# Class 0's V rows gathered per token and summed on TensorE; its routing kept on chip; classes 1 and 2 routed one after the other

## The chip, the core and the metric

One core of one Trainium2 chip runs the kernel. The time is the device time of one execution, in microseconds (us). Engines are named as in the profile: PE is TensorE, DVE is VectorE, ACT is ScalarE, POOL is GpSimd, SP is SyncE.

## The reference

One layer over 512 tokens of width 1024: a token-mixing part, then a channel-mixing part that looks up neurons by product keys (PEER), then a last RMSNorm. All in float32. Cut to what matters here:

```python
h = rmsnorm(x, norm_mix_g); proj = h @ w_in          # u/v gating, q for 3 patterns, k, v, two gates
y_a = spatial_gating_mixer(gelu(u, v)); y_b = dilated_attention_mixer(q, k, v)
x = x + (sigmoid(gate_a) * (y_a @ w_branch_a) + sigmoid(gate_b) * (y_b @ w_branch_b)) @ w_out
h2 = rmsnorm(x, norm_ffn_g)
s = scores of h2 @ w_q against 8 heads x 2 x 128 sub-keys
top_s, top_i = top_k(s, 16)                          # per half; 16 x 16 sums, again top_k 16 per head
expert, gate = 8 heads x 16 experts of 16384 and their softmax, per token
act = gelu(u_tab[expert] . h2) * gate                # 128 rows of 1024 per token
x = x + sum_k act[k] * v_tab[expert[k]]              # 128 rows of 1024 per token
out = rmsnorm(x, norm_final_g)
```

## The kernel before

**Classes.** The 512 tokens are split by t mod 4 into four classes of 128 tokens, one token a partition. Class 0 goes through the whole mixing part first and alone, with plain float32 matmuls (`exact=True`). Classes 1 to 3 follow together, with each operand split into two parts (`split`, L83 to 85) and three matmuls instead of one (`mm`, L102 to 108).

**Two ways to do the PEER part.** Classes 1 and 2 (`ND = 2`) are done densely: all 16384 experts' activations are made on PE (`up_pair`, 128 tiles of 128 experts, `gelu` on ACT), multiplied by a gate matrix that is zero where an expert wasn't chosen, and summed with V on PE into PSUM tiles `acc`. The gate matrix is built by `gates` from one-hot matmuls and goes through DRAM (`g_dram`, read back as `gl`). Classes 0 and 3 are done by gathers (`gathered`): for each of a token's 128 experts one indirect DMA, issued by POOL (L251), brings 128 rows of 4 KB, one for each token, into one of seven `row` buffers. For U, DVE multiplies the row by h2 and sums it (L266); for V, DVE adds the row, scaled by its activation, to `xg` (L259). Both classes are 256 gathers each.

**Routing.** `route` finds one chunk's (two heads') 16 best experts on DVE: top 16 of 128 twice for each head, 50 sums, top 16 of them, and three instructions on 800 elements to look up the expert's number. Four chunks make a class. Classes 0 and 3 write their scores to DRAM (`s_dram`) and `gathered` reads them back; classes 1 and 2 are routed within the loop over scores, chunk by chunk, both classes in turn (`route_of`).

**Order.** `gathered` is a generator, and each `yield` is a step. The two classes make one list: 36 steps of routing, 256 gathers, and again the same for class 3. The 36 of class 0 are emitted ahead of the attention of classes 1 to 3. All later ones are emitted by `gather_steps(us, behind)`, which the projections, the heads, the up tiles and the V loop call behind one of their instructions with the PE time of their piece: it takes `us * rate` steps. `rate` is MIX (0.5) up to the scores, and then what is left of 549 steps over the time of the up tiles and the V loop. `tc.issue_after` puts a step's instructions behind the given one on that one's engine. A planner that simulates the program then fixes each engine's order; every engine runs its own list in that order.

**Stages.** x, norm, transposes to hT (two buffers for `h`); projections z, k, v; class 0's attention, gating, merge, residual, scores; then, for classes 1 to 3, `attention`, `gating`, `merge`, `residual`, `scores` with routing. Then the up tiles ahead of time: 40 kept in SBUF (`pre`), 20 spilled to `a_dram` (`NSP`), beside `gates` for both classes at a high priority. Then the V loop over 128 tiles in pairs: the other 68 up tiles, gl, the product, four float32 matmuls for the first tile of a pair and twelve split ones for the second. `finish` norms each class and stores it. Tile names in rows: `pj` a projection's PSUM, `po` the attention's output (64 of 128 columns a head), `tr` a transpose, `pu_t` an up tile, `pg` a gates tile, `h_dram`, `s_dram`, `x_dram` the tensors in DRAM.

Of the kernel before, what the change touches and what calls it, by code (L numbers as in the profile page):

```python
# [19 lines left out]
P = 128  # L20
# [3 lines left out]
D = 1024  # L24
# [10 lines left out]
NSP = 20  # L35
# [6 lines left out]
GPB = 7  # L42
STEPS = 549
MIX = 0.5
WUS = 4.2
HUS = 4.5
UUS = 3.43
# [4 lines left out]
def body(ctx, tc, a, out):  # L52
# [21 lines left out]
    s_dram = [dp.tile([4, P, 4, P], F32, name=f"s_dram{i}") for i in range(2)]  # L74
    h2_dram = [dp.tile([P, D], F32, name=f"h2_dram{i}") for i in range(2)]
# [25 lines left out]

    def mm(ps, l, r, first, last):  # L102
        if len(l) == 1:
            nc.tensor.matmul(ps, l[0], r[0], start=first, stop=last)  # L104
# [3 lines left out]
        nc.tensor.matmul(ps, l[1], r[0], start=False, stop=last)  # L108
# [120 lines left out]
    def gathered(gp, i, r):  # L229

        h2g = gp.tile([P, D], F32, tag="h2g", name="h2g", bufs=1)
        nc.sync.dma_start(h2g, h2_dram[i])
        xg = gp.tile([P, D], F32, tag="xg", name="xg", bufs=1)
        nc.sync.dma_start(xg, x1_dram[r])
        bv = gp.tile([P, 8, 16], F32, tag="bv", name="bv_g", bufs=1)
        ef = gp.tile([P, 8, 16], F32, tag="ef", name="ef_g", bufs=1)
        for c in range(4):
            sg = gp.tile([P, 4, P], F32, tag="sg", name="sg", bufs=1)
            nc.sync.dma_start(sg, s_dram[i][c])
            yield from route(gp, sg, bv[:, 2 * c:2 * c + 2, :], ef[:, 2 * c:2 * c + 2, :],  # L240
                             lambda: gp.tile([P, D], F32, tag="row", name="eq", bufs=GPB)[:, 0:16 * NC].rearrange(
                                 "p (k n) -> p k n", k=16))
        eidx = gp.tile([P, P], I32, tag="eidx", name="eidx", bufs=1)
        gate = gp.tile([P, P], F32, tag="gate", name="gate", bufs=1)
        nc.vector.tensor_copy(eidx, ef.rearrange("p h k -> p (h k)"))
        softmax16(bv, gate)
        pend = []

        def row_of(table, k):
            row = gp.tile([P, D], F32, tag="row", name="row", bufs=GPB)  # L250
            nc.gpsimd.indirect_dma_start(out=row, out_offset=None, in_=table,  # L251
                                         in_offset=bass.IndirectOffsetOnAxis(ap=eidx[:, k:k + 1], axis=0))
            return row

        def down():
            k0, act = pend.pop(0)
            for k in range(GB):
                row = row_of(a["v"], k0 + k)
# [3 lines left out]
        for k0 in range(0, P, GB):  # L262
            ab = gp.tile([P, GB], F32, tag="ab", name="ab", bufs=2)
            for k in range(GB):
                row = row_of(a["u"], k0 + k)
                nc.vector.scalar_tensor_tensor(row, row, 1.0, h2g, op0=ALU.mult, op1=ALU.mult,  # L266
                                               accum_out=ab[:, k:k + 1])
                yield
# [9 lines left out]

    ph = ExitStack()
# [3 lines left out]
    with ExitStack() as p1:  # L283
        pp = pool(p1, "pp", 4, space=PSUM)
        pst = pool(p1, "pst", 1, space=PSUM)
        ptr = pool(p1, "ptr", 1, space=PSUM)
        pv = pool(p1, "pv", 1, space=PSUM)
# [28 lines left out]
        pa = ExitStack()  # L316
        pha = ExitStack()
        hap = pool(pha, "hap", side="right")
        hA = Op(hap, [P, KT, P], "hA", True)
        with ExitStack() as p0:  # L320
# [67 lines left out]
        aw = pool(pa, "aw", 2, reuse_waits="tile")  # L388

        def attention(pl, cl, x, ybT, exact, hook):  # L390
# [10 lines left out]
            def heads(hp):  # L401
                q1, q2 = q_of(hp)
                po = pv.tile([P, 512], F32, tag="pv", name="po")
                for j, r in enumerate(cl):
                    tok = slice(j * P, j * P + P)
                    for hh in range(2):
# [8 lines left out]
                        sm = aw.tile([P, 768], F32, tag="sm", name="sm")  # L415
                        mx = sp.tile([P, 1], F32, tag="mx", name="mx")
                        nc.vector.tensor_tensor_reduce(out=sm, in0=s[:, 0:768], in1=bias[:, j, :], scale=1.0,
# [4 lines left out]
                        pr = aw.tile([P, 768], F32, tag="pr", name="pr")  # L422
                        nc.scalar.activation(pr, sm, AF.Exp, bias=nb, scale=slope, accum_out=den)
# [9 lines left out]
                        pt = aw.tile([P, 4, P], F32, tag="pt", name="pt")  # L433
# [61 lines left out]
        def residual(pl, cl, mT, exact, hook):  # L495
# [10 lines left out]
            for j, r in enumerate(cl):  # L506
                nc.sync.dma_start(x1_dram[r], x1[:, j, :])
                h2 = pl.tile([P, D], F32, tag="h2", name="h2")
# [4 lines left out]
        def scores(pl, x, n, each, exact, hook):  # L513
            for c in range(4):
                skc = pl.tile([P, 4, P], F32, tag="sk", name="skc")
# [13 lines left out]
        def to_dram(pl, i):  # L529
            def each(c, j, ps):  # L530
                ssb = pl.tile([P, 4, P], F32, tag="ssb", name="ssb")
                nc.scalar.copy(ssb, ps)
                nc.sync.dma_start(s_dram[i][c], ssb)
            return each


        with ExitStack() as ga:
# [5 lines left out]
            m_ = pool(ga, "mA", 2, reuse_waits="tile")  # L543
# [4 lines left out]
            for r, h2 in residual(m_, [0], mT, True, 0):  # L548
                nc.sync.dma_start(h2_dram[0], h2)
                for q in range(2):  # L550
                    t = transpose4([h2[:, (4 * q + i) * P:(4 * q + i + 1) * P] for i in range(4)])
                    h2A.put((slice(None), slice(4 * q, 4 * q + 4), slice(None)), t)
            scores(m_, lambda kt: h2A[:, kt, :], P, to_dram(m_, 0), True, 0)
# [258 lines left out]
```

## Time and profile before

| | us |
|---|---|
| median of three runs (1855.36 to 1861.1) | 1859.0 |
| the profiled execution | 1855.0 |
| its span, first to last instruction | 1853.2 |
| PE busy, weight loads busy, DVE busy | 1651.0, 1345.7, 1300.8 |
| ACT busy, POOL busy | 548.2, 689.5 |
| moved by DMA | 552.5 MB, 298 GB/s on the mean |

Busy times are of instructions and overlap between engines. A busy PE isn't a PE at its peak: a matmul at the half clock takes twice as long. The time between the span and the execution, 1.8 us, lies around the first and last instruction.

### The profile page before, as it was taken

Reading aid. Unit: us, or ns where it says so; the run is one execution under the profiler, and the core shown is the slowest. Engines: PE = TensorE matmul, PEld = TensorE weight load, DVE = VectorE, ACT = ScalarE, POOL = GpSimd, SP = SyncE. Lnnn points to the kernel's source line nnn. Section 1 sums busy time; section 2 is a strip of 40 time slices with the busy share of each in tenths; the row PEclk is TensorE's granted clock in tenths of the full one; section 3 lists DMA queues with packets and bytes.
Section 4 is the critical chain, followed back from the end, with each engine's and each line's share of the span. In section 5 each row is a group of like instructions: output and inputs, shape, how many; then the busy total and the mean of one; then the engine's idle time right before and its main releaser. Section 6 shows DMA issues by size and latency. Waiting matters only on the chain.

```text
span 1853.2 us, 22603 instructions
## 1 busy us (share of the span) xinstructions
PE 1651.0 (89%) x7838; PEld 1345.7 (73%) x7838; DVE 1300.8 (70%) x2749; ACT 548.2 (30%) x1045; POOL 689.5 (37%) x535
## 2 busy tenths in 40 slices
PE   7999989988779977889999865899998999999997
PEld 6988969876679957888779753455566667677675
DVE  3333014999899988999999964687775656667564
ACT  4324113443333323311048694112211111111111
POOL 0000000007676655354555000574453454455350
PEclk9999999995699987999999977999999999999999
DMA  5235777219899998879899735999998999999995
GB/s 201 91 106 167 274 245 281 86 53 329 298 338 378 364 353 328 299 281 368 324 360 383 268 129 198 388 406 379 377 395 315 356 373 357 374 382 406 364 358 195
DMA packets 166914, 552.54 MB, mean 298 GB/s; under 512 B 17296, under 2 KB 38800, under 8 KB 165648
## 3 DMA queue, kind: packets, MB, share of 16 engines
q1 hardware_dynamic: 93072, 282.63, 42.1%
q0 software_dynamic: 73728, 268.47, 38.6%
q8 instruction: 62, 1.02, 0.2%
q14 instruction: 52, 0.43, 0.1%
HBM read 524.29 MB, written 26.74 MB: 297 GB/s over the span
## 4 chain that ended last, share of the span: by engine, by line
PE 45%; DVE 22%; issue 15%; DMA 12%; POOL 3%; ACT 2%; SPq 0%; POOLq 0%; DVEq 0%; ACTq 0%
PE pu_t L632 10%; DVE row L266 6%; PE pj L104 6%; PE acc L104 5%; PE pj L108 5%; PE pj L106 5%; PE pj L107 5%; DMA raw<-in_v_dram 4%; DVE xg L259 3%; POOL row L251 3%; DMA row<-in_u_dram,eidx 2%; PE acc L107 2%; PE acc L108 2%; DMA row<-in_v_dram,eidx 2%; PE acc L106 2%
## 5 line engine op out<-in xcount | busy, mean ns | idle before, releaser
L251 POOL DMA_INDIRECT row<-in_u_dram,eidx x256 | 334.1, 1305 | 525.0 <-DVE pr L429 157.9
L251 POOL DMA_INDIRECT row<-in_v_dram,eidx x256 | 343.1, 1340 | 326.5 <-DVE xg L259 133.7
L632 PE MATMUL pu_t<-h2T,raw 128*128 128x256 f32 x2048 | 456.0, 381 | 5.2 <-DMA raw<-in_ut_dram 3.8
L632 PEld LDWEIGHTS pu_t<-h2T,raw 128*128 128x128 f32 x2048 | 390.0, 191 | 62.5 <-issue 6.6
L259 DVE SCALAR_TENSOR_TENSOR xg<-row,act,xg 128x1024 f32<-128x1024 f32 x256 | 327.9, 1281 | 7.9 <-DMA row<-in_v_dram,eidx 4.6
L266 DVE SCALAR_TENSOR_TENSOR row<-row,h2g 128x1024 f32<-128x1024 f32 x256 | 305.8, 1216 | 17.0 <-DMA row<-in_u_dram,eidx 16.8
L85 DVE TENSOR_TENSOR wlo<-raw,whi 128x1024 fp32r<-128x1024 f32 x88 | 107.1, 1218 | 111.0 <-ACT whi L84 110.8
L104 PE MATMUL acc<-raw,ge 128*128 128x512 f32 x352 | 162.6, 605 | 12.3 <-DMA raw<-in_v_dram 12.3
L84 ACT CAST whi<-raw 128x1024 fp32r<-128x1024 f32 x88 | 92.4, 1050 | 223.1 <-PE pj L107 134.2
L104 PEld LDWEIGHTS acc<-raw,ge 128*128 128x128 f32 x352 | 68.0, 194 | 80.8 <-issue 70.6
L106 PE MATMUL acc<-vh,ah 128*128 128x512 f32 x256 | 116.9, 489 | 8.6 <-ACT vh L84 5.3
L143 POOL TENSOR_TENSOR rs<-ms,mhalf 128x1 f32<-128x1 f32 x16 | 11.4, 717 | 303.6 <-DVE ms L141 303.6
L107 PE MATMUL acc<-vl,ah 128*128 128x512 f32 x256 | 107.5, 423 | 18.4 <-DVE vl L85 18.4
L633 ACT ACTIVATE ge<-pu_t 128x256 f32<-128x256 f32 x68 | 26.0, 383 | 314.0 <-PE pu_t L632 313.9
L106 PE MATMUL pj<-hT_hi,whi 128*128 128x384 f32 (+1 forms) x320 | 114.2, 357 | 4.6 <-ACT u L462 3.6
L107 PE MATMUL pj<-hT_lo,whi 128*128 128x384 f32 (+1 forms) x320 | 112.7, 352 | 0.0
L85 DVE TENSOR_TENSOR vl<-raw,vh 128x1024 fp32r<-128x1024 f32 x64 | 78.2, 1222 | 49.1 <-ACT vh L84 48.1
L108 PE MATMUL pj<-hT_hi,wlo 128*128 128x384 f32 (+1 forms) x320 | 100.6, 357 | 11.6 <-DVE wlo L85 11.5
L108 PE MATMUL acc<-vh,al 128*128 128x512 f32 x256 | 102.5, 408 | 0.9 <-DVE al L85 0.9
L666 PE MATMUL pg<-hot 128*128 128x128 f32 x512 | 74.9, 307 | 31.4 <-ACT stg L669 21.0
L84 ACT CAST vh<-raw 128x1024 fp32r<-128x1024 f32 x64 | 66.8, 1043 | 116.4 <-DMA raw<-in_v_dram 114.5
L666 PEld LDWEIGHTS pg<-hot 128*128 128x128 f32 x512 | 70.5, 216 | 36.6 <-ACT stg L669 29.8
(215 smaller groups left out, 2651.7 us busy)
## 6 DMA issues: line engine op xcount, KB each, us to landing
raw<-in_ut_dram SPq DMA_DIRECT2D x128, 512.0 KB, 6.6
raw<-in_v_dram SPq DMA_DIRECT2D x128, 512.0 KB, 7.1
raw<-in_w_in_dram SPq DMA_DIRECT2D x88, 512.0 KB, 4.1
raw<-in_wq_dram SPq DMA_DIRECT2D x32, 512.0 KB, 5.7
g_dram<-stg SPq DMA_DIRECT2D x8, 2048.0 KB, 7.2
gl<-g_dram SPq DMA_DIRECT2D x32, 512.0 KB, 8.3
raw<-in_wa_dram SPq DMA_DIRECT2D x16, 512.0 KB, 5.5
raw<-in_wo_dram SPq DMA_DIRECT2D x16, 512.0 KB, 5.1
```

Of the source, the lines that this page charges most:

```text
L84: nc.scalar.copy(hi, src)
L85: return nc.vector.tensor_tensor(lo, src, hi.bitcast(F32), ALU.subtract)
L104: nc.tensor.matmul(ps, l[0], r[0], start=first, stop=last)
L106: nc.tensor.matmul(ps, l[0], r[0], start=first, stop=False)
L107: nc.tensor.matmul(ps, l[0], r[1], start=False, stop=False)
L108: nc.tensor.matmul(ps, l[1], r[0], start=False, stop=last)
L251: nc.gpsimd.indirect_dma_start(out=row, out_offset=None, in_=table, in_offset=bass.IndirectOffsetOnAxis(ap=eidx[:, k:k + 1], axis=0))
L259: nc.vector.scalar_tensor_tensor(xg, row, act[:, k:k + 1], xg, op0=ALU.mult, op1=ALU.add)
L266: nc.vector.scalar_tensor_tensor(row, row, 1.0, h2g, op0=ALU.mult, op1=ALU.mult, accum_out=ab[:, k:k + 1])
L632: nc.tensor.matmul(ps, raw[:, kt * P:kt * P + P], h2T.t[0][:, kt, :], start=kt == 0, stop=kt == KT - 1)
L633: last = nc.scalar.activation(dst(k), ps, AF.Gelu)
L666: nc.tensor.matmul(ps[:, m, :], hot[1][:, 4 * q + m, :], hot[0][:, 4 * q + m, :], start=True, stop=True)
```

## The change

Class 0 gets a generator of its own, `gathered_pe`. Its U rows are gathered as before (128 steps). Then the activations and expert numbers are transposed on PE, so that a token's 128 experts lie on the partitions, and a V gather brings the 128 rows of *one token*. Its sum over experts is a matmul with one column of weights; four tokens, one of each quarter of 32 columns, make a group: weights `ex` of 32 columns with one column filled, four tokens, two halves of 512 columns, eight float32 matmuls, accumulated over 32 groups in PSUM. Class 0's scores are copied into a row buffer and routed chunk by chunk within its own loop over scores. Class 1 is routed in the loop over scores, class 2 (`late`) between the gates of class 1 and of class 2. Class 3 keeps the old way, with all its steps in the V loop. Steps are put behind the last matmul on PE as well. Buffers: eight row buffers instead of seven, one `h` buffer in the first stage, `sm` and `pr` of the attention one tile, 12 spilled up tiles instead of 20, the pools of PSUM for the attention closed after it to make room for `acc_A`. The diff, cut:

```diff
-NSP = 20
+NSP = 12
-GPB = 7
-STEPS = 549
-MIX = 0.5
+GPB = 8
+MIX = 0.53
+PUS = 4.4
...
-        with tc.issue_after(behind.ins):
+        with tc.issue_after(behind.ins), tc.issue_after(on_pe.ins):
...
+    def gathered_pe(bv, ef, h2g, r):
+        eidx = gp.tile([P, P], I32, tag="eidx", name="eidx")
+        gate = gp.tile([P, P], F32, tag="gate", name="gate")
+        e = ef.rearrange("p h k -> p (h k)")
+        nc.vector.tensor_copy(eidx, e)
+        softmax16(bv, gate)
+        act = gp.tile([P, P], F32, tag="ab", name="act")
+        yield from u_rows(eidx, h2g, act, 0, P)
+        nc.scalar.activation(act, act, AF.Gelu)
+        nc.vector.tensor_tensor(act, act, gate, ALU.mult)
+        ps = v_acc()
+        nc.tensor.transpose(ps[:, 0:P], act, ident)
+        nc.tensor.transpose(ps[:, P:2 * P], e, ident)
+        actT = gp.tile([P, P], F32, tag="gate", name="actT")
+        nc.scalar.copy(actT, ps[:, 0:P])
+        eT = gp.tile([P, P], I32, tag="eidx", name="eT")
+        nc.vector.tensor_copy(eT, ps[:, P:2 * P])
+        pend = []
+        def down():
+            n, rows, ex = pend.pop(0)
+            for f in range(2):
+                for j in range(4):
+                    c = slice(f * 512, f * 512 + 512)
+                    nc.tensor.matmul(ps[32 * j:32 * j + 32, c], ex[:, j, :], rows[j][:, c], start=n == 0, stop=n == 31)
+        for n in range(32):
+            ex = gp.tile([P, 4, 32], F32, tag="ex", name="ex", bufs=3)
+            one = iota[:, 0:32].unsqueeze(1).to_broadcast([P, 4, 32])
+            nc.vector.scalar_tensor_tensor(ex, one, float(n), actT[:, n:P:32].unsqueeze(2).to_broadcast([P, 4, 32]),
+                                           op0=ALU.is_equal, op1=ALU.mult)
+            rows = []
+            for j in range(4):
+                rows.append(row_of(a["v"], eT[:, 32 * j + n:32 * j + n + 1]))
+                if j == 3 and pend:
+                    down()
+                yield
+            pend.append((n, rows, ex))
+        xg = load_x(r)
+        down()
+        for q in range(2):
+            f = slice(q * 512, q * 512 + 512)
+            nc.vector.tensor_tensor(xg[:, f], xg[:, f], ps[:, f], ALU.add)
+        finish(gp, r, xg)
...
+    NA, NCL = 256, 292
...
-                h = x0.tile([P, D], F32, tag="h", name="h")
+                h = x0.tile([P, D], F32, tag="h", name="h", bufs=1)
...
-                        sm = aw.tile([P, 768], F32, tag="sm", name="sm")
+                        pr = pl.tile([P, 768], F32, tag="pr", name="pr", bufs=3)
...
+            def route_A(c, j, ps):
+                sg = in_row("sg", 4, P)
+                nc.scalar.copy(sg, ps)
+                for _ in route(gp, sg, bvA[:, 2 * c:2 * c + 2, :], efA[:, 2 * c:2 * c + 2, :], row_eq):
+                    pass
...
+        steps = gathered_pe(bvA, efA, h2A_n, 0)
...
+        pat.close()
+        pva = ExitStack()
+        acc_A.append(pool(pva, "pva", 1, side="right", space=PSUM, reuse_waits="tile").tile([P, D], F32, name="acc_A"))
...
         def route_of(c, j, ps):
...
-            if j < ND:
-                for _ in route(l2, ssb, bvs[j][:, 2 * c:2 * c + 2, :], efs[j][:, 2 * c:2 * c + 2, :],
+            if j == 0:
+                route_now(j, c, ssb)
+            elif j == 1:
+                late.append((j, c, ssb))
             else:
-                nc.sync.dma_start(s_dram[1][c], ssb)
+                nc.sync.dma_start(s_dram[c], ssb)
...
-    rate = (STEPS - taken) / (P * UUS + P // 2 * sum(VUS) - LATE)
+    npre = len(KEPT) + len(SPILLED)
+    rate = (NA - taken) / (2 * npre * PUS - LATE)
...
         for r in range(ND):
+            if r == 1:
+                for args in late:
+                    route_now(*args)
             g = l2.tile([P, P], F32, tag="g", name="g")
...
     pr_.close()
+    for _ in steps:
+        pass
+    pva.close()
+    pacc = pool(ctx, "pacc", 1, space=PSUM, reuse_waits="tile")
+    steps = gathered(3)
+    rate = NCL / ((P - 2 * npre) * UUS + P // 2 * sum(VUS) - LATE)
```

## Rows read from the trace of the kernel before

**Rows 1.** The page's parts 1 and 2: busy times; the span in 40 slices.

```profile
PE 1651.0 (89%) x7838; PEld 1345.7 (73%) x7838; DVE 1300.8 (70%) x2749; ACT 548.2 (30%) x1045; POOL 689.5 (37%) x535
...
DVE  3333014999899988999999964687775656667564
...
GB/s 201 91 106 167 274 245 281 86 53 329 298 338 378 364 353 328 299 281 368 324 360 383 268 129 198 388 406 379 377 395 315 356 373 357 374 382 406 364 358 195
```

**Rows 2.** Windows by stage: length, busy PE, PEld, DVE, ACT, POOL, clock, DMA share, GB/s.

```profile
297.00:489.00 192.00, 165.12 (x852) 140.83 (x852) 169.58 (x556) 73.47 (x121) 57.10 (x46) 0.82 0.56 193
489.00:655.00 166.00, 152.54 (x813) 146.87 (x812) 154.93 (x208) 59.59 (x78) 110.38 (x77) 0.97 0.94 344
655.00:712.00 57.00, 34.86 (x128) 25.71 (x127) 45.15 (x61) 16.07 (x23) 30.51 (x25) 0.72 0.96 358
712.00:1056.00 344.00, 323.16 (x1698) 294.65 (x1697) 340.74 (x1025) 126.44 (x277) 159.96 (x114) 0.97 0.88 325
1056.00:1131.00 75.00, 46.30 (x267) 40.39 (x265) 47.66 (x81) 67.94 (x164) 0.00 (x0) 0.82 0.39 153
1131.00:1160.00 29.00, 16.39 (x43) 9.10 (x44) 17.16 (x41) 4.16 (x7) 0.67 (x1) 0.70 0.78 259
1160.00:1836.00 676.00, 634.15 (x2307) 440.77 (x2306) 444.05 (x619) 113.55 (x200) 324.02 (x257) 0.98 0.97 370
```

**Rows 3.** Waits: who waited for whom, us in total, times, the longest.

```profile
DVE pre L718 <- DMA gl<-g_dram: 20.4, 2, 19.7
```

**Rows 4.** Windows of the instructions on tile row alone: DVE, POOL, clock, DMA share, GB/s.

```profile
297.00:489.00 192.00, 47.47 (x71) 57.10 (x46) 0.82 0.56 193
...
489.00:1131.00 642.00, 268.93 (x313) 296.00 (x210) 0.93 0.85 313
```

**Rows 5.** Groups by line: busy us, mean ns of one, idle before.

```profile
L148 ACT ACTIVATE h<-xt 128x1024 f32<-128x1024 f32 x4 | 4.3, 1064 | 4.5 <-DMA xt<-in_x_dram 4.5
...
L259 DVE SCALAR_TENSOR_TENSOR xg<-row,act,xg 128x1024 f32<-128x1024 f32 x256 | 327.9, 1281 | 7.9 <-DMA row<-in_v_dram,eidx 4.6
...
L200 DVE TENSOR_TENSOR eq<-eq,cande 128x800 f32<-128x800 f32 x32 | 30.7, 979 | 0.0
...
L157 DVE MAX8 tv<-rep 128x8 f32<-128x128 f32 x64 | 17.8, 279 | 0.1
...
L661 ACT ACTIVATE hot<-hot,tt 128x128 f32<-128x128 f32 x256 | 78.3, 389 | 17.9 <-DVE hot L658 17.9
...
L669 ACT COPY stg<-pg 128x512 f32<-128x512 f32 x64 | 62.7, 1057 | 6.7 <-PE pg L666 6.6
```

**Rows 6.** Timeline of PE and DVE at the start: start, us, instruction, idle before it.

```profile
5.59 0.15 DVE L141 TENSOR_SCALAR ms<-ss 128x1 f32<-128x1 f32 x1 [4.74 <-ACT h L148]
...
7.82 1.97 PE L292 MATMUL tr<-ident,h 128*128 128x128 f32 x8 [7.82 <-DVE h L331]
...
19.25 1.94 PE L292 MATMUL tr<-ident,h 128*128 128x128 f32 x8 [2.50 <-DVE h L331]
```

**Rows 7.** Timeline of ACT, DVE and POOL from 268 to 415.

```profile
272.51 0.58 ACT L532 COPY ssb<-ps 128x512 f32<-128x512 f32 x1 [2.50 <-PE ps L526]
...
296.54 1.22 DVE L85 TENSOR_TENSOR wlo<-raw,whi 128x1024 fp32r<-128x1024 f32 x1 [38.50 <-ACT whi L84]
...
309.52 0.88 DVE L154 MAX8 tv<-sg 128x8 f32<-128x128 f32 x4 [1.03 <-DMA sg<-s_dram]
...
414.63 1.13 POOL L251 DMA_INDIRECT row<-in_u_dram,eidx  x1 [157.91 <-DVE pr L429]
```

**Rows 8.** Chain that ended last, in order of time: start, us, what.

```profile
447.27 2.29 DVE row L266 x4
...
1208.99 3.43 PE acc L104 x8
...
1360.58 3.45 PE pu_t L632 x16
```

**Rows 9.** Timeline of PE in the attention.

```profile
359.14 1.09 PE L436 MATMUL po<-pt,v_sb 128*64 128x128 f32 x8
```

More of the change, by code (lines that the diff above doesn't have):

```diff
@@ L100, in __getitem__ @@
             return [t[at] for t in self.t]
+    on_pe = None
     def mm(ps, l, r, first, last):
+        nonlocal on_pe
         if len(l) == 1:
-            nc.tensor.matmul(ps, l[0], r[0], start=first, stop=last)
+            on_pe = nc.tensor.matmul(ps, l[0], r[0], start=first, stop=last)
             return
@@ L107, in mm @@
         nc.tensor.matmul(ps, l[0], r[1], start=False, stop=False)
-        nc.tensor.matmul(ps, l[1], r[0], start=False, stop=last)
+        on_pe = nc.tensor.matmul(ps, l[1], r[0], start=False, stop=last)
     steps = iter(())
@@ new lines, in in_row, with row_eq, routed, load_x @@
+    def in_row(name, k, n):
+        row = gp.tile([P, D], F32, tag="row", name=name, bufs=GPB)
+        return row[:, 0:k * n].rearrange("p (k n) -> p k n", k=k)
+    def row_eq():
+        return in_row("eq", 16, NC)
+    def routed():
+        return [gp.tile([P, 8, 16], F32, tag=t, name=t + "_g") for t in ("bv", "ef")]
+    def load_x(r):
+        xg = gp.tile([P, D], F32, tag="xg", name="xg")
+        nc.sync.dma_start(xg, x1_dram[r])
+        return xg
+    def u_rows(eidx, h2g, ab, k0, n):
+        for k in range(n):
+            row = row_of(a["u"], eidx[:, k0 + k:k0 + k + 1])
+            nc.vector.scalar_tensor_tensor(row, row, 1.0, h2g, op0=ALU.mult, op1=ALU.mult, accum_out=ab[:, k:k + 1])
+            yield
@@ L245, in gathered @@
+    def gathered(r):
+        h2g = gp.tile([P, D], F32, tag="h2g", name="h2g")
+        nc.sync.dma_start(h2g, h2_dram)
+        bv, ef = routed()
+        for c in range(4):
+            sg = in_row("sg", 4, P)
+            nc.sync.dma_start(sg, s_dram[c])
+            yield from route(gp, sg, bv[:, 2 * c:2 * c + 2, :], ef[:, 2 * c:2 * c + 2, :], row_eq)
+        eidx = gp.tile([P, P], I32, tag="eidx", name="eidx")
+        gate = gp.tile([P, P], F32, tag="gate", name="gate")
         nc.vector.tensor_copy(eidx, ef.rearrange("p h k -> p (h k)"))
@@ L246, in gathered @@
         softmax16(bv, gate)
+        xg = load_x(r)
         pend = []
[L249 to L253, printed above, removed]
         def down():
@@ L262, in gathered @@
         for k0 in range(0, P, GB):
[L263 to L268, printed above, removed]
+            ab = gp.tile([P, GB], F32, tag="abk", name="ab", bufs=2)
+            yield from u_rows(eidx, h2g, ab, k0, GB)
             act = gp.tile([P, GB], F32, tag="act", name="act", bufs=3)
@@ L277, in gathered @@
         yield
+    NA, NCL = 256, 292
+    gp = pool(ctx, "gp", 1, side="right", reuse_waits="tile")
     ph = ExitStack()
@@ L547, in body, with v_acc @@
             h2A = Op(ya_, [P, KT, P], "h2A", True)
[L548 to L549 removed]
+            for r, h2A_n in residual(m_, [0], mT, True, 0, lambda: gp.tile([P, D], F32, tag="h2g", name="h2g")):
                 for q in range(2):
[L551 removed]
+                    t = transpose4([h2A_n[:, (4 * q + i) * P:(4 * q + i + 1) * P] for i in range(4)])
                     h2A.put((slice(None), slice(4 * q, 4 * q + 4), slice(None)), t)
[L553 to L564 removed]
+            bvA, efA = routed()
+            def route_A(c, j, ps):
+                sg = in_row("sg", 4, P)
+                nc.scalar.copy(sg, ps)
+                for _ in route(gp, sg, bvA[:, 2 * c:2 * c + 2, :], efA[:, 2 * c:2 * c + 2, :], row_eq):
+                    pass
+            scores(m_, lambda kt: h2A[:, kt, :], P, route_A, True, 0)
+        acc_A = []
+        def v_acc():
+            return acc_A[0]
+        steps = gathered_pe(bvA, efA, h2A_n, 0)
         GROUP = [1, 2, 3]
```

95 lines of the change are left out of this document (36 added, 59 removed).

## The prediction

> **What bounds the kernel now.** I read the page first: TensorE (PE) is busy 89% of the span, VectorE (DVE) 70%, and neither share says which of them ends a stage. The slices, 46.3 us each and counted from 0, do [rows 1]: DVE stands at 8 or 9 from slice 7 to slice 22 and mostly at 4 to 7 after that; the DMA engines move 280 to 406 GB/s from slice 9 on, except in slices 22 to 24 and the last.
>
> The stages by windows [rows 2] are then, in us from the span's start. 297 to 489, attention of classes 1 to 3: DVE 169.6 busy of 192, PE at a mean clock of 0.82. 489 to 655, gating and merge: DVE 154.9 and PE 152.5 of 166, both nearly full. 655 to 712, residual: neither is full (PE 34.9, DVE 45.2 of 57); the chain x1, sum of squares, rs, h2, transposes runs in series. 712 to 1056, scores, routing, up tiles, the first gates: DVE 340.7 of 344, PE 323.2. 1056 to 1131: a tail in which ScalarE scales and stores the gates, 67.9 of 75, while PE does 46.3 and no gather is issued. 1131 to 1836, the V loop: first 29 us with PE at 16.4, a wait of 19.7 us for the first gl [rows 3] in it, then PE 634 of 676 with the DMA engines at 0.97 and 370 GB/s.
>
> So DVE sets the time from 297 to 1056, the gates on ScalarE set it to 1131, and PE and DMA share it after that. GpSimd's count [rows 4] puts 46 gathers before 489 and 210 before 1131: 256, so all of class 0 lie there and all of class 3 behind.
>
> **The change, part by part.** The sum is made against the profiled execution, 1855.0 us, of which the span is 1853.2; the median of the three runs, 1859.0, lies 4 us above it, so I give the sum and add 1 to 2.
>
> *Start.* With one h buffer the square of the next class, which writes its junk there, waits for the transposes of the one before. Now the four classes' transposes start from 7.82 to 19.25, 3.8 apart on the mean. In series a class costs its square, 1.06 [rows 5], from ms to the transposes 7.82 - 5.59 = 2.23, the transposes 1.97 [rows 6], and gaps, 5.6; the last starts near 24.7, and nothing hides it, since the first projection needs all classes: +5.5 (between 0 and +9).
>
> *Class 0's routing, in SBUF.* It loses the trip of the scores through DRAM and starts when the first chunk is copied out, at 273.1, not at 309.5; DVE has been idle for 38.5 us by then [rows 7]. One chunk of routing is six instructions on 800 elements (0.98 each), twenty on 128 (0.28, [rows 5]), and some forty smaller ones that I put at 0.08 to 0.2: 17 us, a class 68. About 24 us of it move into idle DVE time, and the gathers, which begin at 414.6, begin near 360.
>
> *Attention.* Its DVE work was 169.6 = 47 for rows [rows 4] + 68 routing + 54 of its own. It becomes 44 + 54 + rows. The hooks of this stage (12 of 4.2 us, 24 of 4.5) ask for 158.4 x 0.53 = 84 u rows at 1.15 (2.29 for two rows, [rows 8]) = 97, so 195 of DVE work where 170 was: it ends near 495, not 489, but with 84 rows done where 46 were. +6. If the rows slide later it gains, see the rivals. The merged sm and pr tile costs nothing: three buffers where two of each stood, and DVE is the limit beside it.
>
> *The V sums.* 128 instructions of 1281 ns leave DVE [rows 5], 164 us by the mean, 147 as they pack. What comes is 32 small ones on 128 elements, 0.28 each by the nearest row, 9 us, and a few evacuations. From 489 to 1131 DVE had 588 us of work; without the 147, the 68 of class 3's routing and the 43 of the 37 rows that come earlier, and with the 9, some 340 are left, so DVE is no bound there. What is late next is PE: each group of four tokens adds 8 float32 matmuls of 512 columns, 16 passes, since a float32 matmul is issued as two (eight passes in 3.43 for four matmuls, 0.429 a pass, [rows 8]). Every matmul behind them on PE's queue waits, and a group whose rows are late would hold the projections; with 8 row buffers a group's gathers are issued one group (4 steps, 7.5 us at 0.53) before they are needed, and a row's 0.5 MB passes in 1.4 us at the stage's 370 GB/s, four in 5.6. I take that as covered.
>
> The price of a group isn't in the trace. The nearest rows are the attention's po, matmuls on one half of the columns: eight passes of 128 columns in 1.09 [rows 9], 0.107 a pass by the columns (0.429 / 4), so a narrower block is not faster, plus about 0.2 around it. They all follow one another in the same half, so they don't say whether different quarters run beside each other. Bounds: all 16 passes in turn, 6.86 + 0.2 = 7.06 a group, 226 us in all; four quarters side by side, 4 passes, 1.72 + 0.2 = 1.92, 61.5 us. I take the low end: the matmuls of the four quarters share neither columns, weights nor output rows, and PE does run what shares nothing side by side, weight loads 73% of the span beside matmuls of 89% [rows 1]. Both ends are kept for the range.
>
> The Trainium skill (TensorEngine Tiling (Array Packing), Theoretical Speedup) gives up to 4 times for at most 32 columns; by it a group is 6.86 / 4 = 1.72 and the whole 55, an estimate that no run here shows yet.
>
> *489 to 1131.* PE is busy 557 of 642 in the four stages summed [rows 2], idle 85. Idle that goes, because DVE no longer ends these stages: 20.8 from 712 to 1056, 28.7 in the gates' tail, 10 of 13.5 in gating and merge; and about 10 from the half clock of the tail (46.3 busy at 0.82). The tail goes because class 1 alone is routed beside the scores (68 where 136 were), its gates run under the up tiles, and class 2 is routed beside them. ScalarE's chain, twice 85 (16 rounds a class, eight scalings of 0.39 and two copies of 1.06 each, [rows 5], 5.2 a round), then ends near 1030, inside the up tiles. The residual's 22 stays. Sum -70. Eight up tiles fewer (NSP 12): 8 x 3.45 [rows 8] = -28, moved to the V loop. The V groups +62. Together -36: the V loop starts near 1106.
>
> *V loop.* +28 for the eight up tiles; -20 for the wait for gl, which now finds the gates written. It still holds 256 gathers, but class 3's routing (36 steps at 292 / 641 = 0.456 a us) takes its first 79 us, in which no row is asked for and the loads draw about 190 GB/s. The bytes were 250 + 7.5 MB [rows 2]; eight more ut loads and eight fewer spilled tiles make 261. 15 of them pass in the first 80 us, 246 in the rest, at 390 GB/s (between the stage's 370 and the 406 of its best slice, [rows 1]) 630: 710 where 705 were, +5. PE's own work, 634 + 16 + 28 = 678, lies under it. Bounds 686 (406 GB/s) and 745 (370).
>
> Sum: 1855.0 + 5.5 + 6 - 36 + 5 = 1835.5; predicted for the median 1836.
>
> **The rivals.**
> (a) *The passes pair up.* The two passes of one matmul use the same quarter and follow each other on PE's queue, and the next quarter's first pass stands behind the second. If the queue starts passes strictly in order, only second pass and next first pass overlap: 9 x 0.429 + 0.2 = 4.06 a group, 130 in all, 68 more than I took, all of it on PE, which ends these stages: 1904, slower. It decides from 2.5 us a group: above 81 us in all the gain is gone. For it: passes of one matmul always stand together. Against: no row shows different quarters.
> The Trainium skill (TensorE: Matmul & The Clock Gate, The mechanism) says that matmuls start and end strictly in program order; that speaks for (a), and no row here contradicts it.
> (b) *No overlap at all*: 226, +164, 2000.
> (c) *The V loop pays it back.* The gathers of class 3 start 80 us into it and at 370 GB/s it takes 745: +35, 1871. For it: DMA at 0.97 in this stage already. Against: its best slice moves 406.
> (d) *The u rows slide out of the attention* into the merge, where DVE now has room: it then ends near 450, 1790. For it: in the kernel before only 46 of the 79 rows that its hooks asked for (158.4 x 0.5) were done by 489. Against: they are done early when they have landed early.
> That the routing doesn't start earlier would cost the 24 us again, 1860; for that DVE would have to be held in its idle 38 us, and nothing holds it.
>
> **How the numbers follow.** Forecast 0.45, (a) 0.24, (b) 0.09, (c) and the late routing 0.10, (d) or more 0.12. A difference under 0.3% (5.6 us) can't be told from none. Around the forecast, 1836 with 1805 to 1856 as its own range, nearly all is faster, (d) too; of (a) one tenth is no worse than before: faster 0.56, same 0.08, slower 0.36. From 1788 to 1915 lie the forecast, (c), two thirds of (a) and of (d): 0.8.
>
> **What would show it.** The first gather near 360; DVE under 20 us of 25 between 500 and 1100; a group of 16 V passes in about 1.9 us (4 shows (a), 7 shows (b)); no stretch of PE at 0.8 clock with ScalarE full ahead of the V loop, which starts near 1106; GpSimd idle for the loop's first 80 us and the loop 710 long. A group at 4 us, or PE waiting for rows of v, makes the prediction wrong.

## The result, and the profile after

The changed kernel takes 1876.6 us (median of 4 runs, 1870.6 to 1877.6); the kernel before took 1860.1 on the same chip. The ratio is 1.0086, 95% interval 1.0057 to 1.0115: slower by 0.9%, where the forecast was 1836, faster by 1.2%. The time lies inside the range given, with the wrong sign. The profiled execution took 1870.6 us, its span 1868.8.

The page of the changed kernel, parts 1 and 2, to be laid beside [rows 1]:

```profile
PE 1703.2 (91%) x8352; PEld 1349.4 (72%) x8352; DVE 1169.3 (63%) x2649; ACT 540.7 (29%) x1031; POOL 643.2 (34%) x535
...
PE   5999987888769998899999998989898989999997
...
DVE  3333118899999343488954338877666657676574
...
GB/s 180 90 99 163 253 256 209 166 364 345 298 295 319 330 312 357 239 290 230 239 246 247 271 357 256 178 411 390 392 317 371 389 370 381 351 393 399 374 392 194
```

The whole result stands in the first line. PE was busy 1651.0 of 1853.2 us and idle 202.2; now it is busy 1703.2 of 1868.8 and idle 165.6. PE's work grew by 52.2 and its idle time shrank by 36.6: 15.6 us lost. VectorE lost 131 us of work and falls to 3 or 4 tenths in seven slices; PE stands at 8 or 9 tenths in these.

The windows of the changed kernel by stage, columns as in [rows 2]:

```profile
0.00:312.00 312.00, 274.41 (x1730) 245.72 (x1731) 104.28 (x292) 82.02 (x168) 5.78 (x16) 0.99 0.53 178
312.00:531.00 219.00, 168.48 (x842) 142.72 (x840) 209.46 (x533) 67.44 (x112) 128.33 (x99) 0.80 0.80 286
531.00:700.00 169.00, 165.65 (x935) 146.36 (x935) 105.61 (x176) 56.15 (x76) 86.39 (x70) 0.97 0.88 318
700.00:757.00 57.00, 45.26 (x216) 29.82 (x215) 21.43 (x30) 15.73 (x22) 21.14 (x23) 0.86 0.92 345
757.00:853.00 96.00, 95.01 (x607) 81.30 (x605) 62.73 (x238) 28.42 (x43) 32.05 (x32) 0.99 0.77 268
853.00:1076.00 223.00, 222.64 (x1315) 187.94 (x1316) 144.23 (x435) 159.06 (x371) 39.39 (x32) 1.00 0.67 241
1076.00:1123.00 47.00, 43.79 (x214) 33.38 (x213) 17.35 (x48) 5.94 (x17) 4.30 (x5) 0.96 1.03 366
1123.00:1200.00 77.00, 71.85 (x215) 41.84 (x214) 66.72 (x287) 16.61 (x23) 0.00 (x0) 0.96 0.61 219
1200.00:1852.00 652.00, 610.35 (x2272) 437.08 (x2271) 433.32 (x608) 106.36 (x194) 324.78 (x257) 0.97 0.96 370
```

PE's idle time (length minus busy) goes stage by stage, before [rows 2] and after, from 24.7 to 37.6 ahead of the attention (before: 272.27 busy of 297), from 26.9 to 50.5 in the attention, from 85.1 to 19.7 between it and the V loop, from 54.5 to 46.8 in the V loop, and stays at 11 in the tail. So the tail of the gates did go. The attention got longer (192 to 219, with VectorE busy 209.5 of it), the stretch behind it shorter (642 to 592), the V loop longer (705 to 729).

One group of V sums in the timeline of PE (start, us, instruction):

```profile
631.03 0.33 PE L111 MATMUL pj<-hT_hi,wlo 128*128 128x384 f32 x1
631.30 1.92 PE L285 MATMUL acc_A<-row,ex 128*32 128x512 f32 x16
633.15 0.44 PE L109 MATMUL pj<-hT_hi,whi 128*128 128x384 f32 x1
```

Sixteen passes and the next matmul 1.85 us after the first. The windows of the instructions on tile row alone (PE, PEld, DVE, POOL) give the sum, and the rows that answer to [rows 4]:

```profile
312.00:531.00 219.00, 0.00 (x0) 0.00 (x0) 114.87 (x192) 128.33 (x99) 0.80 0.80 286
531.00:1123.00 592.00, 67.78 (x512) 14.03 (x512) 37.97 (x66) 181.02 (x157) 0.98 0.80 287
```

The V sums cost PE 67.8 us (six of the 32 groups stand in two parts with other matmuls between them, which costs about 1 us each, see below), and 96 u rows (two instructions each) of 1.20 us lie in the attention. The wait that answers to [rows 3] did not shrink:

```profile
DVE pre L795 <- DMA gl<-g_dram: 36.1, 3, 29.7
```

### The profile page after: what moved, and what is told of

Same layout as the page of the kernel before. It is cut to its first block, busy times and chain, and to the rows that moved or that the text cites. A ratio compares the mean times of both kernels' runs of the same rounds, so it can differ in the third digit from the quotient of the medians.

```text
span 1868.8 us, 23296 instructions
## 1 busy us (share of the span) xinstructions
PE 1703.2 (91%) x8352; PEld 1349.4 (72%) x8352; DVE 1169.3 (63%) x2649; ACT 540.7 (29%) x1031; POOL 643.2 (34%) x535
## 4 chain that ended last, share of the span: by engine, by line
PE 34%; DMA 9%; DVE 5%; issue 4%; POOL 2%; ACT 1%; SPq 1%; POOLq 0%; DVEq 0%; ACTq 0%
PE pu_t L107 18%; PE acc L107 6%; DMA raw<-in_v_dram 4%; PE pg L733 3%; DMA raw<-in_ut_dram 2%; PE acc L110 2%; PE acc L111 2%; POOL row L234 2%; PE acc L109 2%; DMA row<-in_u_dram,eidx 1%; DVE vl L85 1%; PE acc_A L285 1%; DMA ge<-a_dram 1%; DMA sg<-s_dram 0%; SPq L779 0%
## 5 line engine op out<-in xcount | busy, mean ns | idle before, releaser
L107 PE MATMUL pu_t<-h2T,raw 128*128 128x256 f32 x2048 | 464.7, 383 | 8.0 <-DMA raw<-in_ut_dram 6.7
L234 POOL DMA_INDIRECT row<-in_u_dram,eidx x256 | 339.8, 1327 | 348.3 <-DVE eidx L265 92.8
L234 POOL DMA_INDIRECT row<-in_v_dram,eT x128 | 133.2, 1040 | 354.8 <-PE acc_A L285 311.4
L234 POOL DMA_INDIRECT row<-in_v_dram,eidx x128 | 160.6, 1255 | 183.4 <-DVE xg L326 78.5
L326 DVE SCALAR_TENSOR_TENSOR xg<-row,act,xg 128x1024 f32<-128x1024 f32 x128 | 164.3, 1284 | 8.1 <-DMA row<-in_v_dram,eidx 6.0
L725 DVE TENSOR_TENSOR hot<-iota,tt 128x1024 f32<-128x1024 f32 x64 | 75.4, 1222 | 56.0 <-issue 49.7
```

Of the source, the lines that this page charges most:

```text
L107: on_pe = nc.tensor.matmul(ps, l[0], r[0], start=first, stop=last)
L326: nc.vector.scalar_tensor_tensor(xg, row, act[:, k:k + 1], xg, op0=ALU.mult, op1=ALU.add)
L725: nc.vector.tensor_tensor(hot[k], iota.unsqueeze(1).to_broadcast([P, 8, P]), tt[:, k, c0:c0 + 8].unsqueeze(2).to_broadcast([P, 8, P]), ALU ...
```

## The experiments

Ratios are to the kernel before, run on the same chip, with 95% intervals. "V on VectorE" means that class 0's V rows are summed by 128 multiply-adds again, everything else as changed.

**The V sums alone undone.**

```
-        ps = v_acc() ... transposes, one-hot ex, down()
+        xg = load_x(r)
+        for k in range(P):
+            row = row_of(a["v"], eidx[:, k:k + 1])
+            nc.vector.scalar_tensor_tensor(xg, row, act[:, k:k + 1], xg, op0=ALU.mult, op1=ALU.add)
+            yield
```

> Only the sum of class 0's V rows is undone: 128 multiply-adds of 1.15 us on VectorE in place of 512 matmuls; the routing, the order, the buffers and the rates stay as in the changed kernel. Theory A (PE bounds the stretch from the attention to the V loop, 572 busy of 592, and VectorE has 240 us free): PE loses 66 us, VectorE takes 147, both fit, the stretch shortens by 30 to 60, whole time 1820 to 1850; then the move to PE itself was a loss and the gain of the stretch came from the routing in turn. Theory B (VectorE bounds as soon as it has the sums): the stretch is as long as in the kernel before, 630 to 645, whole time 1910 to 1930, and the move to PE is worth some 50.

Measured: 1846.3 us, 0.9922 (0.9895 to 0.9949). (The PE version has 256 matmuls; 512 is the number of their passes.) Its windows from the attention's end to the V loop:

```profile
541.00:660.00 119.00, 112.69 (x624) 110.93 (x625) 110.95 (x163) 46.80 (x65) 86.91 (x57) 0.98 0.94 347
660.00:749.00 89.00, 67.72 (x311) 57.20 (x310) 78.34 (x83) 26.33 (x36) 55.88 (x39) 0.87 0.96 368
749.00:831.00 82.00, 80.79 (x485) 80.51 (x484) 78.71 (x177) 28.88 (x43) 45.61 (x32) 0.97 0.88 314
831.00:1050.00 219.00, 209.54 (x1114) 187.72 (x1115) 187.03 (x537) 116.86 (x277) 44.18 (x35) 0.98 0.69 252
1050.00:1102.00 52.00, 43.79 (x242) 38.95 (x241) 24.69 (x24) 46.46 (x111) 0.56 (x1) 0.84 0.57 213
```

PE is idle 46.5 of 561 us here, 19.7 of 592 in the changed kernel, 85.1 of 642 before. The other edits already take 39 of the 85 away; putting the V sums on PE takes 27 more and pays 68 for it. Theory A holds: the kernel that is faster than before is the one without the edit that the title names first.

**A square of two edits: V on PE or VectorE, class 2 routed in turn or at once.**

```
-            if j == 0:
+            if j < ND:
                 route_now(j, c, ssb)
-            elif j == 1:
-                late.append((j, c, ssb))
```

> The changed kernel with one edit undone: class 2 is routed beside the scores together with class 1, as before, instead of later; the V sums stay on PE. Together with the next run (the same edit with the V sums on VectorE) and the two that exist it makes a square of two edits. Theory A (routing in turn is what takes the tail of the gates away, whoever sums the V rows): the gates of class 1 start 60 us later, ScalarE's chain of twice 85 us runs out behind the up tiles again, the V loop starts 20 to 40 later: 1895 to 1915. Theory B (with the V sums on PE, VectorE is free enough that both classes are routed in time): within 8 of 1876, and the order of the routing is worth nothing.

> V sums on VectorE and class 2 routed at once: of the change only class 0's routing in SBUF, the smaller spill and the smaller buffers are left. Theory A (routing in turn alone brought the gain of the version at 1846): 1865 to 1885, no faster than the kernel before, with PE idle in a tail of 25 to 40 us ahead of the V loop. Theory B (the gain came from class 0's routing in SBUF and its earlier gathers): 1843 to 1853.

| | in turn | at once |
|---|---|---|
| V on PE | 1.0086 (1.0057 to 1.0115) | 1.0143 (1.0077 to 1.0208), 1882.2 us |
| V on VectorE | 0.9922 (0.9895 to 0.9949) | 1.0187 (1.0124 to 1.0251), 1891.9 us |

Routing in turn is worth 2.7% (some 49 us) with the V sums on VectorE, and nothing certain with them on PE (intervals overlap). The move to PE makes no certain difference when class 2 is routed at once, and costs 1.6% (30 us) when it is routed in turn. Each edit frees VectorE for the gates; done together, the second is paid for and finds nothing to free. Of the theories, B of the first run holds (1882.2, within 8 of 1876) and A of the second, though 7 us over its range. The windows of the lower right corner show what either edit removes, PE waiting beside a full ScalarE (68.9 of 75); the line below them, of the upper right corner, shows that with the V sums on PE nothing of it is left, PE 366.9 of 369 from the scores to the V loop:

```profile
738.00:1050.00 312.00, 285.29 (x1535) 262.25 (x1536) 251.61 (x699) 123.55 (x262) 88.02 (x67) 0.96 0.71 253
1050.00:1125.00 75.00, 53.77 (x309) 47.14 (x307) 40.35 (x37) 68.86 (x168) 0.56 (x1) 0.86 0.49 190
...
751.00:1120.00 369.00, 366.92 (x2146) 305.75 (x2146) 215.54 (x703) 195.00 (x431) 79.64 (x69) 0.99 0.72 257
```

**Routing in turn alone, on the kernel before**, and the same with the smaller spill (NSP 20 to 12). The edit is that of the change to route_of, with its buffers.

> The kernel before with one edit of the change: class 2 is routed after class 1's gates instead of with class 1 (its scores wait in four buffers of their own, the routing's tiles are single). Theory A (this edit alone takes away the tail of the gates, in which PE is busy 46 of 75 us at 0.82 clock, and half of the wait for the first gl): 1815 to 1840. Theory B (VectorE, full from 712 to 1056 with the V sums on it, only moves the routing behind the other work, and it needs class 0 in SBUF to gain): 1850 to 1865.

> The same with 12 up tiles spilled instead of 20. In the changed kernel 20 instead of 12 cost 16 us with the V sums on PE and 13 with them on VectorE. Theory A (the spill's price is that the loop gets only 13 us shorter by eight up tiles that cost 28 ahead of it): 10 to 16 us faster than the run before. Theory B (here the up tiles ahead of the loop stand beside ScalarE's gates and cost nothing): 10 to 25 us slower than the run before.

Measured: 1850.7, 0.9958 (0.9934 to 0.9981), and 1883.9, 1.0127 (1.0089 to 1.0166). So the single edit is not worth 49 everywhere; here it is worth some 8, which is theory B. The windows of the first:

```profile
712.00:1056.00 344.00, 326.28 (x1698) 296.37 (x1699) 341.74 (x1019) 126.83 (x278) 163.36 (x114) 0.96 0.90 330
1056.00:1131.00 75.00, 48.57 (x274) 42.47 (x272) 48.23 (x89) 67.23 (x163) 0.00 (x0) 0.84 0.41 158
```

VectorE stays full to 1056 and the tail stays [rows 2]: what VectorE has to do ahead of the gates is as much as before, in another order. That class 0's earlier routing and u rows make the difference to the changed kernel is argued, not shown by a run of its own. With 12 spilled, PE is idle 76 of these 419 us, 44 with 20: the up tiles had filled the wait, and without them it is bare. That run is 33 us slower, the way of theory B but more than its 10 to 25; the V loop took the eight tiles in at more than their own 28 us, 737 for 700.

**The spill alone, in the changed kernel** (NSP 12 to 20).

> The changed kernel with one number undone: 20 up tiles spilled instead of 12, so that eight up tiles move from the V loop ahead of it. Theory A (with the V sums on PE, PE is full on both sides of the V loop's start, 3.6 us idle in the 270 ahead of it): the loop starts 28 to 32 us later and is 24 to 32 shorter, whole time 1868 to 1880. Theory B (the loop is bound by its transfers, which change by 8 MB less than their spilled tiles): it is only 5 to 10 shorter, whole time 1890 to 1900.

> V sums on VectorE and 20 up tiles spilled. Ahead of the V loop PE waits here for ScalarE's scaling of the gates (PE 35 and 27 busy of 40 us from 1050 to 1130). Theory A (the eight up tiles fill this wait): the loop starts 5 to 15 later and is 24 to 32 shorter, whole time 1823 to 1838. Theory B (VectorE, nearly full until 1050, keeps the gates as late behind the up tiles as before): the loop starts 25 later, whole time 1842 to 1850.

Measured: 1892.4, 1.0182 (1.0121 to 1.0244), and 1859.1, 1.0005 (0.9977 to 1.0032). The windows of the first, ahead of the V loop and the loop itself:

```profile
852.00:1152.00 300.00, 294.19 (x1680) 246.82 (x1679) 161.93 (x484) 170.85 (x400) 43.16 (x40) 1.00 0.74 266
1152.00:1873.00 721.00, 657.53 (x2381) 454.93 (x2380) 499.18 (x896) 120.59 (x210) 326.70 (x258) 0.97 0.92 352
```

Eight up tiles add 30 us ahead of the loop and take only 8 (729 to 721) out of it. PE's busy time in the loop falls by the 25 that they are, but its idle time grows from 46.8 to 63.5. So theory B is right on this loop: most of an up tile in it passes in the time in which PE waits for rows and loads. It is no rule of the V loop. With V on VectorE eight up tiles fewer left it no shorter (733 us with 12 spilled, 740 with 20), and that run came out 9 us over the slower of its theories; on the kernel before, as said, the eight cost 37. What sets the loop's length beside PE's own work stays open.

**The V loop without class 3's gathers, and with its routing moved ahead of it.**

```
-                row = row_of(a["v"], eidx[:, k0 + k:k0 + k + 1])
-                nc.vector.scalar_tensor_tensor(xg, row, act...
+                nc.vector.scalar_tensor_tensor(xg, still, act...        # one row of zeros; the u rows likewise
```

> Leaves out class 3's 256 gathers: the same multiply-adds read one row of zeros instead, so that class 3's result is not computed; everything ahead of the V loop is unchanged. It halves the loop's bytes (258 to 124 MB). Theory A (the loop is bound by its transfers at 370 GB/s): it becomes PE's 682 us minus the waits for data, some 640 to 665, whole time 1785 to 1812. Theory B (the loop is bound by PE, and the eight up tiles moved into it are its price): 700 to 725, whole time 1845 to 1872.

> Class 3's 36 routing steps are issued between class 0's last V rows, under the up tiles, instead of in the V loop's first 77 us; nothing else moves. Theory A (the V loop is bound by its DMA at 370 GB/s, and 256 gathers are squeezed into what is left after the routing): its 258 MB then draw 370 GB/s from the start, 258 / 370 = 697 us instead of 729, the routing's 68 us fit beside the up tiles (VectorE 144 of 223 there), whole time 1840 to 1850. Rival B (the V loop is bound by PE, 682 busy of 729, with eight more up tiles than before): it stays above 715, whole time 1865 to 1875. Rival C (VectorE has no room in the up tiles, since class 2 is routed there too): the V loop starts 20 to 30 later, whole time within 8 of 1876.

Measured: 1802.9 (one run) without gathers; 1872.3, 1.0063 (1.0029 to 1.0097) with the routing early. The loop of the first, then of the second:

```profile
1123.00:1200.00 77.00, 71.94 (x221) 42.28 (x220) 68.18 (x296) 16.81 (x23) 0.00 (x0) 0.98 0.62 220
1200.00:1787.00 587.00, 587.00 (x2264) 428.39 (x2263) 439.18 (x599) 108.41 (x193) 0.55 (x1) 1.00 0.53 182
```

```profile
1125.00:1200.00 75.00, 53.65 (x136) 28.48 (x134) 52.09 (x109) 12.81 (x19) 37.65 (x29) 0.86 1.04 402
1200.00:1854.00 654.00, 628.54 (x2347) 449.97 (x2348) 406.71 (x547) 109.59 (x199) 296.69 (x229) 0.98 0.94 354
```

Without gathers PE is full at clock 1.00 and the loop takes some 665 instead of 729. So the gathers cost 65 us, 0.25 us each: about 40 in idle PE, the rest in PE's busy time, which goes from 659 to 682 at a mean clock of 0.97. But that price isn't paid because they start late: with the routing gone from the loop's first 77 us they start at once, at 402 GB/s, PE falls to 54 of 75, and the loop stays at 729. Theory A of the second run fails: an earlier start of the gathers is no remedy.

**Fewer u rows in the attention.**

```
+            rate = 0.2
             attention(pool(gq, "qB", 2, reuse_waits="tile"), GROUP, hB, ybT, False, WUS)
+            rate = MIX
```

> One number is changed: during the attention of classes 1 to 3 the hooks ask for 0.2 steps a microsecond instead of 0.53 (about 32 u rows instead of 84); the rest are done later. Theory A (the attention is bound by VectorE, 209 busy of 219 us, because 96 u rows of 1.15-1.2 us lie in it): some 50 rows fewer take 60 us of VectorE work out, the stage ends when PE's 168 us are done and takes 165 to 180 us, and since VectorE has 240 us free behind it nothing is given back before the V loop: whole time 1825 to 1840. Rival B (the merged sm and pr tile, worked in place, or the wait of each step for PE's matmul makes a head slow): VectorE's load falls but the stage stays at 205 to 219 us, whole time 1865 to 1877. Rival C (the rows are only moved): the stage shrinks, the stretch from it to the V loop grows by as much, whole time 1870 to 1880.

Measured: 1868.3, 1.0065 (1.0040 to 1.0089).

```profile
312.00:503.00 191.00, 161.04 (x841) 137.34 (x841) 154.91 (x432) 67.52 (x112) 63.52 (x53) 0.85 0.61 206
503.00:640.00 137.00, 132.33 (x723) 129.65 (x724) 122.17 (x199) 48.23 (x66) 96.50 (x60) 0.98 0.89 328
640.00:712.00 72.00, 51.59 (x213) 39.78 (x213) 57.41 (x93) 22.95 (x33) 33.73 (x26) 0.85 0.91 337
712.00:807.00 95.00, 95.00 (x589) 81.39 (x589) 62.13 (x235) 26.49 (x39) 32.26 (x32) 0.97 0.75 260
807.00:1121.00 314.00, 303.67 (x1763) 230.10 (x1762) 164.17 (x495) 165.66 (x390) 102.27 (x89) 0.98 0.89 324
```

The attention is 28 us shorter, so VectorE was its bound; at 191 it no longer is (154.9 busy), and its length is that of before. Yet the loop starts at 1121, not 1123: the V sums that stood in the merge now stand in the up tiles, and PE's idle time in the residual and the up tiles goes from 15 to 31. In whole it is nearly theory C: 8 us less than the changed kernel, which the intervals of the two ratios (1.0040 to 1.0089, 1.0057 to 1.0115) can't tell from none.

**Two looks at the groups on PE.** First the order of the eight matmuls, both halves of a quarter in a row; then the changed kernel without the wait that holds each step behind PE's last matmul:

```
-            for f in range(2):
-                for j in range(4):
+            for j in range(4):
+                for f in range(2):
```

```
-        with tc.issue_after(behind.ins), tc.issue_after(on_pe.ins):
+        with tc.issue_after(behind.ins):
```

> Only the order of the eight V matmuls of a group changes: both halves of one quarter of the columns, then of the next, instead of the first half of all four quarters and then the second. If PE starts whatever quarter is free, whatever the order, a group of 16 passes stays at 1.85 us and the time at 1871 to 1877. If passes start in the order of the queue and one that waits for its quarter holds those behind it, four passes of a quarter stand in a row and only the last overlaps the next quarter's first: 13 x 0.429 = 5.6 us a group, 32 groups 178 instead of 66, time 1960 to 1990.

> The changed kernel without the wait of each step's place in the order for the last matmul of PE issued ahead of it; all else stays. Theory A (the attention is long because 96 rows lie in it, and the wait only orders): within 6 of 1876, the attention 212 to 222. Theory B (the wait puts rows between a head's instructions on VectorE and makes its chain long): the attention falls below 205, whole time 1855 to 1868.

Measured: 1881.5 (one run), and 1900.2, 1.0228 (1.0189 to 1.0268). Timelines of PE, first the one (a whole group, then one that other matmuls split), then the other:

```profile
918.44 1.94 PE L285 MATMUL acc_A<-row,ex 128*32 128x512 f32 x16
920.32 0.92 PE L107 MATMUL pu_t<-h2T,raw 128*128 128x256 f32 x3
...
637.92 1.93 PE L285 MATMUL acc_A<-row,ex 128*32 128x512 f32 x12
639.78 0.45 PE L109 MATMUL pj<-hT_hi,whi 128*128 128x384 f32 x1
...
641.04 1.90 PE L285 MATMUL acc_A<-row,ex 128*32 128x512 f32 x4
642.88 0.45 PE L109 MATMUL pj<-hT_hi,whi 128*128 128x384 f32 x1
```

```profile
905.15 1.05 PE L285 MATMUL acc_A<-row,ex 128*32 128x512 f32 x4
906.13 3.72 PE L107 MATMUL pu_t<-h2T,raw 128*128 128x256 f32 x16
909.78 1.05 PE L285 MATMUL acc_A<-row,ex 128*32 128x512 f32 x2
```

The order changes nothing in a group: 1.88 us. The split group shows why: twelve passes, all of three quarters, take 1.86 us, and the four of the last quarter alone take 1.84. The passes of one quarter follow one another, those of different quarters run beside each other, and the fullest quarter sets the time.

The second run fits neither theory. The attention got no shorter (its last output matmul begins at 532.4, in the changed kernel at 527.7), so the wait isn't what made it long. But without the wait the planner spreads a group's matmuls among others: the sums stand in 68 parts instead of 38, and a part of two passes takes PE 1 us by itself, as one of four does and one of eight. The sums cost 97.6 us instead of 67.8, and the kernel 1.4% more. The low price is that of eight matmuls that stand together.

**Towards the fastest.** V on VectorE, with 0.3 steps a microsecond in the attention; with 20 spilled as well; with the first h in a free row buffer as well (twice); h alone with 12 and 0.53; and the middle (16, 0.4, h):

```
-                h = x0.tile([P, D], F32, tag="h", name="h", bufs=1)
+                h = gp.tile([P, D], F32, tag="row", name="h", bufs=GPB)
```

> V sums on VectorE and 0.3 steps a microsecond in the attention (48 rows instead of 84). Theory A (the attention is bound by VectorE only above some 190 us, PE's chain of heads sets the rest): the attention goes from 229 to 195-200 us; the 36 rows later cost 43 us of VectorE, for which the up tiles have 60 free: whole time 1820 to 1838. Theory B (what is taken out of the attention comes back behind it, as with the V sums on PE, where 28 us became 8): 1838 to 1848.

> As the one before, with 0.3 steps a microsecond in the attention (48 rows instead of 84). The attention is 25 shorter; with 12 spilled this went back into a tail of the gates (PE 28 and 31 busy of 40 us from 1050 to 1130) and into a longer V loop. Theory A (the up tiles fill that tail): the loop starts near 1095 and takes 720 to 728, whole time 1812 to 1830. Theory B (ScalarE's chain of the gates sets the loop's start, and it needs VectorE for its one-hot tiles first): as without the fewer rows, 1828 to 1840.

> The same, and the first h of each class takes one of the eight row buffers, which are empty at the start, instead of the one buffer of its own. Theory A (the single buffer costs the start 6.5 us, first projection matmul at 27.5 instead of 21.0): first matmul back at 20.5 to 21.5, whole time 5 to 8 less than the run before. Theory B (the start's 6 us are hidden behind the loads of the first weights): no difference above 3 us.

> The changed kernel with the V sums on VectorE (12 spilled, 0.53 steps in the attention) and the first h of each class in a row buffer. Theory A (the start's single buffer delays all that follows, 7 us as in the run with 20 spilled): 1836 to 1842, the fastest so far. Theory B (here the gates' tail takes the 7 us back): 1844 to 1850.

> V sums on VectorE, h in row buffers, 16 up tiles spilled and 0.4 steps a microsecond in the attention: halfway between the two versions that ran at 1842 (20 spilled, 0.3) and 1852 (12 spilled, 0.53). Theory A (idle time ahead of the loop, 32 to 40 us in the two stages, is lost either way, and the sum has a flat minimum): 1838 to 1850. Theory B (with 16 the up tiles end when the gates do, and both the tail and the longer loop go): 1820 to 1835.

> The fastest version so far once more, nothing changed, for an interval on the same chip as the run before: 1836 to 1848, faster than the kernel before by 0.6 to 1.2% and than the changed kernel by 1.5 to 2%.

Measured, in this order: 0.9962 (0.9929 to 0.9995); 0.9943 (0.9912 to 0.9975); 0.9906 (0.9876 to 0.9935); 0.9952 (0.9923 to 0.9981); 0.9927 (0.9900 to 0.9955); 0.9912 (0.9881 to 0.9942). The best, 1842.0 and 1838.4 us, beats the kernel before by 0.9% and by its ratio the changed one by 1.8%. The single h buffer does cost the start 8 us (first projection at 19.3 instead of 27.4), but alone it gave nothing to be seen at 12 spilled. The first two came out some 4 and 8 us over the slower of their theories, the fourth 2. All six lie within 0.6% of each other, a flat minimum: what one of them takes out of a stage ahead comes back as idle time of PE in the up tiles and the V loop (84 to 100 us there in these six, 74 in the first run of this section).

## Why the prediction was wrong, point by point

Stage by stage, in us, the terms of the sum and what came, by the windows above and in [rows 2] (in brackets each stage's length before and after; the start is all that lies ahead of the attention):

| | forecast | measured |
|---|---|---|
| start (297 to 312) | +5.5 | +15 |
| attention (192 to 219) | +6 | +27 |
| between attention and V loop (642 to 592) | -36 | -50 |
| V loop (705 to 729) | +5 | +24 |

The misses, +9.5, +21, -14 and +19, make the 35 us from 1835.5 to 1870.6. So three terms failed, the attention, the V loop and the start; the term that holds the V sums came out better than forecast.

*The price of the V sums* was right: 1.85 us for a whole group for 1.92, 67.8 in all for 61.5, the rest for the six split groups. Rivals (a) and (b) fall. The Trainium skill (TensorEngine Tiling (Array Packing), Theoretical Speedup) gives up to 4 times; 6.86 / 1.85 is 3.7. The Trainium skill's rule of strict program order (TensorE: Matmul & The Clock Gate, The mechanism), which stood beside rival (a), is not borne out by these runs. Strict order would make a group 4.06 us by (a)'s working, and 5.6 with the two halves of a quarter in a row; 1.85 and 1.88 came.

*The stretch between attention and V loop* (-36): 65.5 us of PE's idle time went where the sum had 60 (its other 10 were the half clock's), and the tail with it; the mean clock rose from 0.93 [rows 4] to 0.98. What the sum couldn't show is whose gain it was. It put the removal to the V sums (147 us off VectorE) and to routing in turn at once, and set PE's 61.5 against the whole of it. The square shows that they are two ways to one gain. With the sums left on VectorE I would have had to forecast 39 us of idle time gone at no price on PE; I never priced the change without its main edit.

*The attention term* (+6) counted 84 rows at 1.15 where 96 at 1.20 came: 115 us for 97, and VectorE at 209 for 195. It also took VectorE as all but full, in a stage in which it had been idle for 22 of 192 us [rows 2]. That VectorE bounds it was right; that relief comes back elsewhere is what the experiment adds.

*The start* (+5.5) held for the first projection (+6.4, 27.4 for 21.0), but class 0's part ends 15 us later. The single buffer for h is shown; the rest, single buffers in class 0's stages, was not tried by itself.

*The V loop* (+5) was the longer of two times, PE's 678 or the transfers' 630 + 80. The rate was mis-sized: 370 GB/s, not 390, the bound of rival (c). The picture was wrong too. PE's waits for data come on top of its work (46.8 idle beside 682), and the wait for gl didn't go (36.1, 20.4 before); PE's idle time at the loop's start could fall only from 12.6 to 5, not by the 20 that the prediction took off for it. Of the 24 us, 8 go with the eight up tiles; what the other 16 are no run shows. That rival (c)'s 1871 is the profiled time is luck: it had the loop at 745 and all else as in the forecast.

*First gather* at 358.5 (360 forecast) and GpSimd idle in the loop's first 77 us: both as told. VectorE was to stay under 20 us of 25; from 875 to 950 it was full, beside a full PE.

## What to carry to other kernels

When two edits relieve the same engine, price each with the other already made: their gains need not add, and each is paid for in full. Before moving work onto the engine that is busiest over the whole span, compare its added busy time with the idle time that would remain without the move, not with the idle time of today. Where an engine waits for data, as PE in this V loop, its waits come on top of its work: take their sum from a stage like it, not the maximum of two loads.

## What the runs showed of the hardware

Float32 matmuls of 32 columns in four different quarters ran beside each other: sixteen passes of 512 columns in 1.85 us, for 0.429 a pass of the full width [rows 8], 3.7 at a time. It made no difference whether the queue had one half of all four quarters first or two matmuls of one quarter in a row (1.88). Passes of one quarter went in turn: four of them alone took 1.84 us, as long as twelve of three quarters. So a group that is torn apart loses: 1 us for each part, be it of two passes or of eight. And 256 gathers beside PE's streamed loads made this V loop 65 us longer (664 to 729; the shorter time from one run), 0.25 us each; started 77 us earlier, they left it at 729.
